# The factors for the first rows of W2 are loaded into f's blocks instead of W1's q tiles, and two of them one pass later

## The chip, the core and the metric

The kernel runs on one core of a Trainium2 chip. The metric is the time of one execution on the device in microseconds (us): 2252.89 us for the kernel before, the median of three runs (2249.2 to 2253.3). The profile comes from one execution of its own, of 2253.21 us.

## What is computed

One layer of an encoder trunk for a sequence of 512 rows of 2048 float32 values: an input projection, two kinds of attention (a window with grouped keys, and a dilated one), an output projection, a layer norm, and the part that this case is about:

```python
h = layer_norm(ALPHA * h + mix, ln1_g[i], ln1_b[i])
ff = jnp.square(jax.nn.relu(h @ w1[i])) @ w2[i]
ple = (p[i] @ w_ple[i]) * jax.nn.sigmoid(h @ w_ple_gate[i])
h = layer_norm(ALPHA * h + ff + ple, ln2_g[i], ln2_b[i])
```

W1 has 2048 x 8192 elements, W2 has 8192 x 2048.

## The kernel before

Products with large weights are made in float32r with a split: of each operand a high part (a copy that ScalarE rounds, `wh`, `sh`) and a low part (what VectorE finds left over, `wl`, `sl`), and three matmuls high x high, low x high, high x low.

**Passes and steps.** From the gate's projection on, every product of 512 x 1024 outputs is made by Strassen's scheme with seven products, `strassen` (L602 to L674): two passes for the gate, eight for W1 (chunk n = 0 to 7 of 1024 columns of f), eight for W2 (m = 0 to 3 for the rows of W2, c = 0 and 1 for the halves of its columns). A pass has 28 steps, each a pair (p, k): product p of the seven, and k, a quarter of its depth. `STEPS` sets their order: steps 0 to 11 are products 1, 5 and 6, steps 12 to 19 products 3 and 7 in turn, steps 20 to 27 products 2 and 4. Each step splits one weight tile of 128 x 1024 (`w_split`, L598 on ScalarE and L599 on VectorE) and makes 12 matmuls with it (L668, L670, L671). For product 5 VectorE first forms a difference of two weight tiles (L634) and from it product 6's tile (L635), for 3 and 7 one more (L622), for 4 one more (L617).

**Factors.** The other operand of step (p, k) is a *factor*, `sg[k // 2][p]`: half g = k // 2 of product p, split into high and low (`put`: L532 on ScalarE, L533 on VectorE) and kept for the whole pass. For W1 they are made from h and serve all eight passes. For W2 they are made from f: `squared`, which is called two steps after a quarter of a W1 chunk is complete, puts relu's square into a block f, forms three differences and a sum in place on VectorE (L738 to L745) and stores seven blocks of 512 KB to a DRAM tensor `s_d` (L733, three on ScalarE's queue and four on POOL's). `f_factors(m, ...)` loads those of chunks 2m and 2m + 1 again, 14 blocks per m, each with one DMA on SP's queue (L584) and one split. For a new m the loads are put between the steps of the pass before (the last W1 pass for m = 0, else pass c = 1 of m - 1), two steps behind the last use of the old factor, since a factor has two buffers per product, one for each half; those of products 2 and 4, which are used last, are put into the new m's first pass by the table `LATE`.

**Rings.** All these tiles come from a few rings, whose tags give the number of buffers:

```python
WB = {"r": 4, "q": 2, "k": 4, "wh": 3, "wl": 3, "c": 3, "g": 4}
LATE = {2: (12, 16), 4: (14, 18)}
```

A weight tile for product 5's difference and one for 3's and 7's go through `q`, two buffers (L592 with tag q; from the second W2 pass on, `hold`, they are kept in `g` instead). The f blocks go through `g`, four buffers, and so do a few tiles of the gate's passes. In the kernel before, the loads of factors, `block("qs", "q")`, go through `q`.

**Order.** The text of the program gives the order of steps; a scheduler then orders the instructions on each engine by when it expects them to be ready. Each engine and each DMA queue works through its own list in order, so that an instruction that waits holds all behind it. SP's queue carries the weight tiles of rings r, q and g and the factors; POOL's carries ring k's weights, four of the stores of f's blocks and, in W2, the sums into `z_d`.

Of the kernel before, what the change touches and what calls it, by code (L numbers as in the profile page):

```python
# [38 lines left out]
def block_kernel(ctx: ExitStack, tc: tile.TileContext, xT, pT, positions, w_in, w_o, w_gate, w_ple,  # L39
# [47 lines left out]
    def unit(src, acts, nk=16, mid=None):  # L87
        o = bank()
        for g in range(nk // 8):
            raw = raw_load(src[:, g * 1024:(g + 1) * 1024])  # L90
            for p in range(2):
                piece_mm(o, raw[:, p * 512:(p + 1) * 512], acts, 8 * g + 4 * p, nk)
            if g == 0 and mid:
                mid()
        return o
# [74 lines left out]
    def rope_split(o):  # L170
        raw = t_f("qr", "q")
        nc.scalar.activation(raw, o, AF.Copy)
        sw = t_f("sw", "q", F32, 32)
        nc.vector.stream_shuffle(sw, raw[:32], swap)
        nc.vector.tensor_tensor(sw, sw, sinr, op=ALU.mult)
        nc.vector.tensor_tensor(raw[:32], raw[:32], cosr, op=ALU.mult)
        nc.vector.tensor_tensor(raw[:32], raw[:32], sw, op=ALU.add)
        return split(raw, "q", "q")
# [150 lines left out]
    for h in range(8):  # L329
# [22 lines left out]
        q = rope_split(unit(w[1], x_hl, 16, q_mid))  # L352
# [167 lines left out]
    def w_tile(name, tag, shape=(P, 1024), dt=F32):  # L520
        return wp.tile(list(shape), dt, name=name, tag=tag, bufs=WB[tag])
# [4 lines left out]
    def block(name, tag="g"):  # L526
        return w_tile(name, tag, (P, 4, HS))

    def put(sg, p, src):
        hi = sp.tile([P, 4, HS], R32, name=f"s{p}h", tag=f"s{p}h", bufs=2)  # L530
        lo = sp.tile([P, 4, HS], R32, name=f"s{p}l", tag=f"s{p}l", bufs=2)
        nc.scalar.activation(hi, src, AF.Copy)  # L532
        nc.vector.tensor_tensor(lo, src, hi.bitcast(F32), op=ALU.subtract)  # L533
        sg[p] = hi, lo

    def h_factors(g, sg):

        q = {}

        def get(*ks):  # L540
            for i in ks:
                th, kh = i // 2, i % 2
                k0 = 8 * kh + 4 * g
                q[i] = block("qh")
                nc.sync.dma_start(q[i], h_d[k0:k0 + 4, :, th * HS:(th + 1) * HS].rearrange("k p t -> p k t"))

        def a1():
            get(0, 2, 3)
            put(sg, 1, q[0])

        def a2():
            nc.vector.tensor_tensor(q[3], q[3], q[2], op=ALU.add)
            put(sg, 5, q[3])

        def a3():
            nc.vector.tensor_tensor(q[3], q[3], q[0], op=ALU.subtract)
            put(sg, 6, q[3])

        def b1():
            get(1)  # L560
            put(sg, 2, q[1])

        def b2():
            get(0, 2)
            nc.vector.tensor_tensor(q[2], q[0], q[2], op=ALU.subtract)
            put(sg, 7, q[2])

        def b3():
            get(3)
            nc.vector.tensor_tensor(q[1], q[1], q[3], op=ALU.subtract)  # L570
            nc.vector.tensor_tensor(q[1], q[1], q[2], op=ALU.add)
            put(sg, 3, q[1])

        return [a1, a2, a3], [b1, b2, b3, lambda: put(sg, 4, q[3])]

    def f_factors(m, sg):


        at = {False: {}, True: {}}
        for p in range(1, 8):  # L580
            for g in range(2):
                def step(p=p, g=g):
                    x = block("qs", "q")
                    nc.sync.dma_start(x, s_d[2 * m + g, p - 1])  # L584
                    put(sg[g], p, x)
                late = p in LATE
                at[late].setdefault(LATE[p][g] if late else STEPS.index((p, 2 * g + 1)) + 2, []).append(step)
        return at

    def w_load(src, tag):  # L590
# [105 lines left out]
    early, late = zip(*(h_factors(g, sh[g]) for g in range(2)))  # L696
# [20 lines left out]

    sf = [{}, {}]
    at = f_factors(0, sf)
    for n in range(NFC):  # L720
        f = {}
# [86 lines left out]
    for m in range(NM):  # L808
        more = m < NM - 1
        late = at[True]  # L810
        if more:
            nsf = [{}, {}]
            at = f_factors(m + 1, nsf)
        for c in range(2):
            def read(p, b, c=c):
                e = pair("ev")
                nc.scalar.activation(e, b, AF.Copy)  # L817
                nc.gpsimd.dma_start(z_d[READ[p][0], 2 * c + READ[p][1]], e, accum_op=ALU.add)
            mid = late if c == 0 else at[False] if more else {}
            strassen(lambda k, q, m=m, c=c: w2[m, c, q, k], sf, read if more else last_sum(c), m + c > 0, mid,  # L820
                     STEPS if more or c == 0 else ENDS)
        if more:
            sf = nsf
# [6 lines left out]
STEPS = ((1, 0), (1, 1), (5, 0), (1, 2), (5, 1), (1, 3), (5, 2), (6, 0), (5, 3), (6, 1), (6, 2), (6, 3),  # L830
         (3, 0), (7, 0), (3, 1), (7, 1), (3, 2), (7, 2), (3, 3), (7, 3),
         (2, 0), (4, 0), (4, 1), (2, 1), (4, 2), (4, 3), (2, 2), (2, 3))
LATE = {2: (12, 16), 4: (14, 18)}
# [97 lines left out]
```

## Time and profile before

| what | value |
|---|---|
| median of three runs | 2252.89 us |
| the profiled execution | 2253.21 us, of which the span of instructions 2251.4 us |
| TensorE matmuls | 2144.6 us busy, 95% of the span |
| VectorE | 1608.7 us, 71% |
| ScalarE | 1060.3 us, 47% |
| POOL | 124.3 us, 6% |
| last W1 pass (n = 7) | 1480.75 to 1577.19 us, 96.44 us |
| first W2 pass (m = 0, c = 0) | 1577.19 to 1663.13 us, 85.94 us |
| W1 pass n = 6, for comparison | 1399.95 to 1480.75 us, 80.80 us |

Times are read from the start of the span. The busy time of TensorE is modelled at the end of each matmul, so that what counts is when it starts and where it sits idle. A timeline row gives the start, the length, the engine, the line, the operation and its tiles, and in brackets the idle time of the engine just before it with what ended it. A pass begins with the first matmul on `s1h`.

### The profile page before, as it was taken

The page shows a single profiled execution, that of the slowest core. Times are in us where ns is not written, and L with a number is a line of the kernel's source. Part 1 is how long each engine was busy: PE and PEld are TensorE (multiplying, and loading weights), DVE is VectorE, ACT ScalarE, POOL GpSimd, SP SyncE. Part 2 cuts the span into 40 slices and gives each one's busy share as a digit, 9 for nine tenths or more (in the row PEclk, how much of TensorE's full clock was granted, in tenths as well). Part 3 has the DMA queues.
Part 4 walks back from the last instruction along what each step waited for, and adds up shares of the span by engine and source line. Part 5 has one row for each costly group of instructions (what it writes and reads, how often), then busy time and mean ns, then how long its engine had stood idle before and what let it go on. Part 6 is the DMA issues. An engine that isn't in the chain of part 4 may idle for free.

```text
span 2251.4 us, 26067 instructions
## 1 busy us (share of the span) xinstructions
PE 2144.6 (95%) x9672; PEld 1760.2 (78%) x9672; DVE 1608.7 (71%) x1945; ACT 1060.3 (47%) x1372; POOL 124.3 (6%) x192
## 2 busy tenths in 40 slices
PE   8999999999995699999999999999999999999995
PEld 7888888888884488888888888877777777887784
DVE  7666655566375888776876877777777776777787
ACT  5554444443234444455555455455455455455331
POOL 0000000000003000000000000000011011101000
PEclk9999999999998799999999999999999999999998
DMA  6222222233325875665575566567779679679562
GB/s 226 76 66 75 77 74 85 75 108 128 107 94 185 273 272 194 216 216 196 196 239 174 195 215 202 196 210 235 260 198 282 178 206 279 180 212 294 170 243 103
DMA packets 125696, 405.80 MB, mean 180 GB/s; under 512 B 13152, under 2 KB 24416, under 8 KB 125568
## 3 DMA queue, kind: packets, MB, share of 16 engines
q1 hardware_dynamic: 89696, 289.71, 38.2%
q0 software_dynamic: 23584, 85.06, 13.7%
q10 hardware_dynamic: 12288, 29.36, 3.8%
q8 instruction: 76, 1.25, 0.2%
q14 instruction: 52, 0.43, 0.1%
HBM read 333.82 MB, written 70.25 MB: 179 GB/s over the span
## 4 chain that ended last, share of the span: by engine, by line
PE 76%; DMA 9%; DVE 9%; issue 4%; ACT 2%; DVEq 0%; SPq 0%; ACTq 0%
PE u L71 9%; PE u L72 9%; PE u L73 9%; PE a L668 9%; PE a L670 8%; PE a L671 8%; PE b L671 4%; DVE wl L599 4%; PE b L668 4%; PE b L670 4%; DMA wr<-in_w 4%; PE c L671 2%; PE c L668 2%; PE c L670 2%; DMA qs<-s_d 2%
## 5 line engine op out<-in xcount | busy, mean ns | idle before, releaser
L598 ACT ACTIVATE wh<-wr 128x1024 fp32r<-128x1024 f32 x288 | 303.8, 1059 | 357.9 <-PE a L670 198.8
L599 DVE TENSOR_TENSOR wl<-wr,wh 128x1024 fp32r<-128x1024 f32 x288 | 350.9, 1220 | 111.0 <-ACT wh L598 111.0
L64 ACT ACTIVATE wh<-raw 128x512 fp32r<-128x512 f32 x216 | 135.7, 629 | 283.9 <-PE u L72 271.1
L65 DVE TENSOR_TENSOR wl<-raw,wh 128x512 fp32r<-128x512 f32 x216 | 150.9, 699 | 161.0 <-ACT wh L64 129.3
L598 ACT ACTIVATE wh<-wk 128x1024 fp32r<-128x1024 f32 x144 | 152.5, 1060 | 182.5 <-PE a L670 95.8
L71 PE MATMUL u<-xh,wh 128*128 128x512 f32 x576 | 227.8, 396 | 5.8 <-ACT xh L64 5.8
L72 PE MATMUL u<-xl,wh 128*128 128x512 f32 x576 | 225.8, 392 | 0.0
L73 PE MATMUL u<-xh,wl 128*128 128x512 f32 x576 | 225.7, 392 | 0.0
L599 DVE TENSOR_TENSOR wl<-wk,wh 128x1024 fp32r<-128x1024 f32 x144 | 175.4, 1222 | 62.0 <-ACT wh L598 61.8
L617 DVE TENSOR_TENSOR wk<-wr,wk 128x1024 f32<-128x1024 f32 x72 | 88.1, 1224 | 90.5 <-DMA wr<-in_w 83.5
L668 PE MATMUL a<-wh,s1h 128*128 128x512 f32 x288 | 114.7, 398 | 31.4 <-ACT wh L598 31.2
L71 PEld LDWEIGHTS u<-xh,wh 128*128 128x128 f32 x576 | 108.9, 189 | 27.3 <-ACT xh L64 5.8
L73 PEld LDWEIGHTS u<-xh,wl 128*128 128x128 f32 x576 | 108.8, 189 | 22.7
L72 PEld LDWEIGHTS u<-xl,wh 128*128 128x128 f32 x576 | 108.9, 189 | 22.0 <-DVE xl L65 0.4
L668 PE MATMUL b<-wh,s5h 128*128 128x512 f32 x288 | 116.3, 404 | 8.4 <-ACT wh L598 8.4
L671 PE MATMUL b<-wl,s5h 128*128 128x512 f32 x288 | 117.1, 407 | 7.3 <-DVE wl L599 7.3
L668 PE MATMUL a<-wh,s6h 128*128 128x512 f32 x288 | 113.8, 395 | 4.9 <-ACT ev L817 2.8
L671 PE MATMUL b<-wl,s3h 128*128 128x512 f32 x288 | 113.2, 393 | 5.0 <-DVE wl L599 4.9
L671 PE MATMUL c<-wl,s2h 128*128 128x512 f32 x288 | 113.2, 393 | 4.9 <-DVE wl L599 4.7
L668 PE MATMUL a<-wh,s7h 128*128 128x512 f32 x288 | 113.0, 392 | 4.4 <-ACT wh L598 4.1
L671 PE MATMUL a<-wl,s1h 128*128 128x512 f32 x288 | 113.7, 395 | 2.4 <-DVE wl L599 2.4
L670 PE MATMUL b<-wh,s5l 128*128 128x512 f32 x288 | 115.6, 401 | 0.0
(243 smaller groups left out, 4934.8 us busy)
## 6 DMA issues: line engine op xcount, KB each, us to landing
wr<-in_w SPq DMA_DIRECT2D x196, 512.0 KB, 3.9
wq<-in_w SPq DMA_DIRECT2D x72, 512.0 KB, 3.8
raw<-in_w_in SPq DMA_DIRECT2D x64, 512.0 KB, 3.7
wk<-in_w POOLq DMA_DIRECT2D x64, 512.0 KB, 5.6
qs<-s_d SPq DMA_DIRECT2D x56, 512.0 KB, 4.9
z_d<-ev POOLq DMA_DIRECT2D x42, 512.0 KB, 7.3
raw<-in_w_o SPq DMA_DIRECT2D x32, 512.0 KB, 3.5
s_d<-f POOLq DMA_DIRECT2D x32, 512.0 KB, 4.3
```

What stands on the lines that cost most here:

```text
L64: nc.scalar.activation(hi, src, AF.Copy)
L65: nc.vector.tensor_tensor(lo, src, hi.bitcast(F32), op=ALU.subtract)
L71: nc.tensor.matmul(o, wh, ah, start=start, stop=False)
L72: nc.tensor.matmul(o, wh, al, start=False, stop=False)
L73: nc.tensor.matmul(o, wl, ah, start=False, stop=stop)
L598: nc.scalar.activation(hi, t, AF.Copy)
L599: nc.vector.tensor_tensor(lo, t, hi.bitcast(F32), op=ALU.subtract)
L617: nc.vector.tensor_tensor(t4[k], get(b21, k, 2, "r"), t2[k], op=ALU.subtract)
L668: nc.tensor.matmul(o, sh[:, i, x], wh[:, c], start=first and k == 0 and j == 0, stop=False, skip_group_check=skip)
L670: nc.tensor.matmul(o, sl[:, i, x], wh[:, c], start=False, stop=False, skip_group_check=skip)
L671: nc.tensor.matmul(o, sh[:, i, x], wl[:, c], start=False, stop=k == 3 and j == 1, skip_group_check=skip)
```

## The change

Two things change in `f_factors`. For m = 0 the 14 loads go through ring `g`, the four buffers of f's blocks, and no longer through `q`; for m = 1 to 3 they go through `q` as before. And for m = 0 and half g = 1, products 3 and 7 join the table of late loads: of this half four products (2, 3, 4, 7) are now loaded within the first W2 pass, of the other half two as before. So two loads move from the last W1 pass (steps 20 and 21 of it) to steps 3 or 4 and 6 of the first W2 pass.

```diff
@@ -580,11 +580,12 @@
         for p in range(1, 8):
             for g in range(2):
                 def step(p=p, g=g):
-                    x = block("qs", "q")
+                    x = block("qs", "q" if m else "g")
                     nc.sync.dma_start(x, s_d[2 * m + g, p - 1])
                     put(sg[g], p, x)
-                late = p in LATE
-                at[late].setdefault(LATE[p][g] if late else STEPS.index((p, 2 * g + 1)) + 2, []).append(step)
+                plan = LATE if m or g == 0 else {**LATE, 3: (3, 4), 7: (3, 6)}
+                late = p in plan
+                at[late].setdefault(plan[p][g] if late else STEPS.index((p, 2 * g + 1)) + 2, []).append(step)
         return at
```

**SP's queue, start of the last W1 pass.** Names end in the number of their buffer: wq_11705, 11751, 11799 and 11843 are product 5's second tiles for k = 0 to 3, wr_11648 to 11773 product 1's tiles, qs_11727 the factor (1, g = 0), qs_11793 (5, 0), qs_11821 (1, 1), wr_11929 and 11972 product 3's tiles. Before:

```order
L592 DMA wr_11575<-in_w1 128x1024
L584 DMA qs_11727<-s_d_5213 128x1024
L592 DMA wr_11648<-in_w1 128x1024
L592 DMA wr_11687<-in_w1 128x1024
L592 DMA wr_11733<-in_w1 128x1024
L592 DMA wr_11773<-in_w1 128x1024
L592 DMA wq_11751<-in_w1 128x1024
L592 DMA wr_11929<-in_w1 128x1024
L584 DMA qs_11793<-s_d_5213 128x1024
L592 DMA wq_11799<-in_w1 128x1024
L592 DMA wr_11972<-in_w1 128x1024
L584 DMA qs_11821<-s_d_5213 128x1024
```

The same place with the change:

```order
L593 DMA wr_11575<-in_w1 128x1024
L593 DMA wq_11751<-in_w1 128x1024
L593 DMA wr_11648<-in_w1 128x1024
L593 DMA wr_11687<-in_w1 128x1024
L593 DMA wr_11733<-in_w1 128x1024
L593 DMA wr_11773<-in_w1 128x1024
L593 DMA wq_11799<-in_w1 128x1024
L593 DMA wr_11929<-in_w1 128x1024
L593 DMA wq_11843<-in_w1 128x1024
L584 DMA qs_11727<-s_d_5213 128x1024
L593 DMA wr_11972<-in_w1 128x1024
L584 DMA qs_11793<-s_d_5213 128x1024
```

Every weight tile of ring q moved up by one place in that ring (wq_11751 stands where the first factor stood), and the first factor moved behind all of product 5's tiles.

**ScalarE, the last W1 pass from step 3 on.** wh_11757, 11805 and 11849 belong to steps (5,1), (5,2) and (5,3), wh_11775 to (1,3), wh_11827 to (6,0). Before:

```order
L532 ACTIVATE s1h_11729<-qs_11727 128x1024
L598 ACTIVATE wh_11757<-wr_11687 128x1024
L598 ACTIVATE wh_11775<-wr_11773 128x1024
L598 ACTIVATE wh_11805<-wr_11733 128x1024
L532 ACTIVATE s5h_11795<-qs_11793 128x1024
L598 ACTIVATE wh_11827<-wk_11707 128x1024
```

With the change:

```order
L599 ACTIVATE wh_11757<-wr_11687 128x1024
L599 ACTIVATE wh_11775<-wr_11773 128x1024
L532 ACTIVATE s1h_11729<-qs_11727 128x1024
L599 ACTIVATE wh_11805<-wr_11733 128x1024
L599 ACTIVATE wh_11827<-wk_11707 128x1024
L532 ACTIVATE s5h_11795<-qs_11793 128x1024
```

The first factor's copy moved back by two weight copies and now stands directly ahead of that of step (5,2).

**ScalarE, the first W2 pass.** wh_12451 belongs to step (5,2), wh_12467 to (6,0), `ev` is the copy of product 1's sums out of PSUM, which must be done before product 6 adds to the same bank. Before:

```order
L598 ACTIVATE wh_12451<-wr_12384 128x1024
L598 ACTIVATE wh_12467<-wk_12364 128x1024
L532 ACTIVATE s2h_12561<-qs_12559 128x1024
L817 ACTIVATE ev_12442<-a_12302 128x1024
L598 ACTIVATE wh_12489<-wr_12424 128x1024
```

With the change:

```order
L532 ACTIVATE s3h_12392<-qs_12390 128x1024
L599 ACTIVATE wh_12451<-wr_12372 128x1024
L599 ACTIVATE wh_12467<-wk_12352 128x1024
L532 ACTIVATE s7h_12441<-qs_12439 128x1024
L532 ACTIVATE s2h_12561<-qs_12559 128x1024
L818 ACTIVATE ev_12436<-a_12290 128x1024
```

Three copies of factors instead of one now stand ahead of `ev`, one of them ahead of step (5,2)'s weights.

## Rows read from the trace of the kernel before

**Rows 1.** The page: TensorE's busy time, and the chain that ended last, by engine.

```profile
PE 2144.6 (95%) x9672; PEld 1760.2 (78%) x9672; DVE 1608.7 (71%) x1945; ACT 1060.3 (47%) x1372; POOL 124.3 (6%) x192
PE 76%; DMA 9%; DVE 9%; issue 4%; ACT 2%; DVEq 0%; SPq 0%; ACTq 0%
```

**Rows 2.** Busy time by stretch: whole passes, then their steps 0-11 and 12-19.

```profile
core 0: us, PE busy (x) PEld busy (x) DVE busy (x) ACT busy (x) POOL busy (x), PEclk, DMA share, GB/s
1399.95:1480.75 80.80, 79.96 (x370) 66.30 (x368) 59.52 (x52) 41.48 (x45) 4.25 (x8) 1.00 0.60 202
1480.75:1577.19 96.44, 87.38 (x370) 68.85 (x368) 71.53 (x62) 50.15 (x55) 4.25 (x8) 0.95 0.67 224
1577.19:1663.13 85.94, 81.47 (x346) 65.54 (x344) 61.10 (x53) 40.55 (x41) 9.55 (x14) 0.96 0.82 254
...
1399.95:1433.48 33.53, 33.53 (x153) 27.85 (x152) 28.36 (x25) 16.61 (x18) 2.13 (x4) 1.00 0.58 205
1433.48:1457.09 23.61, 22.77 (x105) 18.68 (x104) 17.33 (x15) 10.59 (x11) 0.00 (x0) 1.00 0.52 165
1480.75:1522.69 41.94, 37.78 (x154) 29.45 (x152) 30.92 (x27) 19.78 (x21) 2.14 (x4) 0.92 0.61 207
1522.69:1553.17 30.48, 25.58 (x103) 19.35 (x102) 23.76 (x21) 15.46 (x17) 0.00 (x0) 0.94 0.64 206
1577.19:1616.68 39.49, 36.72 (x153) 29.87 (x152) 30.72 (x27) 18.38 (x20) 3.90 (x6) 0.91 0.84 280
1616.68:1641.37 24.69, 22.99 (x98) 17.66 (x96) 17.66 (x16) 11.88 (x13) 1.47 (x2) 1.00 0.67 208
1780.76:1804.33 23.57, 22.08 (x98) 17.94 (x96) 12.28 (x11) 10.32 (x11) 1.33 (x2) 1.00 0.62 179
```

**Rows 3.** Timeline of TensorE: the longest stalls of the two passes.

```profile
1500.26 0.64 PE L668 MATMUL b<-wh,s5h 128*128 128x512 f32 x1 [2.05 <-ACT wh L598]
...
1548.30 0.79 PE L668 MATMUL a<-wh,s7h 128*128 128x512 f32 x1 [2.08 <-ACT wh L598]
...
1600.05 0.79 PE L668 MATMUL a<-wh,s6h 128*128 128x512 f32 x1 [2.77 <-ACT ev L817]
```

**Rows 4.** Timeline of VectorE, last W1 pass: what it waited for.

```profile
1497.83 1.23 DVE L634 TENSOR_TENSOR wr<-wq,wr 128x1024 f32<-128x1024 f32 x1 [3.84 <-DMA wq<-in_w]
...
1545.85 1.23 DVE L622 TENSOR_TENSOR wq<-wr,wq 128x1024 f32<-128x1024 f32 x1 [1.57 <-DMA wq<-in_w]
```

**Rows 5.** Timeline of SP's queue, last W1 pass: DMAs as they are issued.

```profile
1478.00 0.33 SPq L592 DMA_DIRECT2D wq<-in_w  x1
...
1484.93 0.33 SPq L584 DMA_DIRECT2D qs<-s_d  x1
1490.61 0.33 SPq L592 DMA_DIRECT2D wq<-in_w  x1
```

**Rows 6.** Timeline of ScalarE's queue and POOL: stores of f's blocks.

```profile
1486.60 0.33 ACTq L733 DMA_DIRECT2D s_d<-f  x1
...
1492.01 0.53 POOL L733 DMA_DIRECT2D s_d<-f  x1 [1.74 <-DVE f L745]
```

**Rows 7.** DMA issues from 1486 to 1501: number, KB each, median us to landing.

```profile
s_d<-f POOLq DMA_DIRECT2D x3, 512.0 KB, 7.9
s_d<-f ACTq DMA_DIRECT2D x1, 512.0 KB, 4.7
wq<-in_w SPq DMA_DIRECT2D x1, 512.0 KB, 7.2
...
qs<-s_d SPq DMA_DIRECT2D x1, 512.0 KB, 3.2
```

**Rows 8.** Timeline of ScalarE, first W2 pass: the wait ahead of product 1's copy.

```profile
1598.03 1.06 ACT L532 ACTIVATE s2h<-qs 128x1024 fp32r<-128x1024 f32 x1 [5.25 <-DMA qs<-s_d]
1598.99 1.00 ACT L817 ACTIVATE ev<-a 128x1024 f32<-128x1024 f32 x1
```

**Rows 9.** DMA issues from 1588 to 1592: the load of that factor, median us to landing.

```profile
qs<-s_d SPq DMA_DIRECT2D x1, 512.0 KB, 7.6
```

## The prediction

> **What bounds the kernel now.** I read the page first: TensorE is busy for 95% of the span and holds 76% of the chain that ended last [rows 1]. So a change gains only where TensorE sits idle or runs at a lower clock. The second view is the busy time by stretch, cut at the passes [rows 2]: the W1 pass n = 6 takes 80.80 us, the last W1 pass, in which ten factors for W2 are loaded, 96.44 us, and the first W2 pass 85.94 us. All three have the same 28 steps. Cut further, the loss sits in four stretches. Steps 0 to 11 take 33.53 us in n = 6, 41.94 us in the last W1 pass (8.41 more) and 39.49 us in the first W2 pass (5.96 more). Steps 12 to 19 take 23.61 us in n = 6 and 30.48 us in the last W1 pass (6.87 more); in the first W2 pass 24.69 us against 23.57 us two passes later (1.12 more). Together 22.36 us: all that these loads can cost.
>
> The loss is half waiting, half clock. In the last W1 pass TensorE is busy for 37.78 of the 41.94 us, and its granted clock is 0.92 on average, against 1.00 in n = 6 [rows 2]: part of the time it runs at the lower of the two levels, 1.2 GHz instead of 2.4, and the matmuls that begin behind the long stalls are recorded at 0.64 to 0.79 us each [rows 3]. At a mean of 0.92, some 3.4 us of the 41.94 (8%) are lost to the clock, beside 4.2 us of idle time.
>
> The third view, the timelines, says what is late. TensorE waits for weight copies by ScalarE (2.05 us at step (5,2), 2.08 at (7,3), the two longest of that pass) [rows 3]; behind them VectorE waits for tiles of ring q, 3.84 and 1.57 us [rows 4]. These come late because factors sit in that ring of two: SP issues the q tile for (5,2) only at 1490.61, 5.7 us behind the factor ahead of it [rows 5], since it needs the buffer of the first factor, which VectorE has only then split. In the first W2 pass the stall is of another kind: step (6,0) waits 2.77 us for the copy of product 1's sums [rows 3], which stands on ScalarE behind the copy of a factor whose load it waits for, 5.25 us [rows 8].
>
> **The change, part by part.** No instruction and no byte is added; the same 14 loads and splits are made, some in another place.
>
> *Steps 12 to 19 of the last W1 pass.* The factors of products 3 and 7 alternate with W1's q tiles in two buffers there; now they take g's. SP can issue the q tiles for (7,0) and (7,1) before their steps. What remains is VectorE's load: 21 instructions in 23.76 us of busy time before, 15 in n = 6 [rows 2]; two factors move away, so 19. At 17.33 / 15 = 1.16 us each that is 22.0 us, under the 23.61 us that TensorE needs, but with little to spare. I take 24.1 us: a gain of 6.4 us. Bounds: 0 (VectorE's order makes the same stalls) and 6.9.
>
> *Steps 0 to 11 of the last W1 pass.* The q tiles now come first: the one for (5,2) is issued at 1478.00, where the one for (5,1) was [rows 5], the one for (5,3) at about 1484.9, where a factor was. Those two waits go. But the first factor now needs a buffer of ring g, and all four hold f blocks of n = 6. The first to be free is the block of quarter (0,0): its store leaves ScalarE's queue at 1486.60 and takes 4.7 us [rows 6, 7]. So the factor is issued at 1491.3, no longer ahead of product 5's tiles. How long it takes is bounded by the rows of the same window: 3.2 us (the fastest factor) to 7.9 us (the stores); I take the q tile's 7.2, issued at 1490.61 among the same stores [rows 7]. It lands at 1498.5. On ScalarE its copy now stands directly ahead of that of step (5,2)'s weights: 1.05 us each, done by 1499.6 and 1500.6. VectorE then makes the factor's low part (to 1500.9), a sum for product 6 (to 1502.0) and only then the low part for (5,2), to 1503.2, at 1.2 us each as in rows 4, some overlapped. In n = 6's rhythm (5,2) would start at 1498.2 (1500.26 less the 2.05 of idle time [rows 3]) and want the low part two matmuls later, at 33.53 / 153 = 0.22 us each [rows 2]: at 1498.7. So it is 4.5 us late, a little more than the idle time of this stretch before (4.2), in one piece instead of several. For the clock I take 2.6 us instead of 3.4, since there is one recovery instead of two. 4.5 + 2.6 = 7.1 against 8.41: a gain of 1.3 us. With a landing in 3.2 us everything is 4 us earlier and the low part 0.5 us late, and the gain is up to 7.7; with 7.9 us and the two further factors late as well I put the lower end at a loss of 2.
>
> The next loads follow the other stores: the last leaves POOL at 1492.01 and needs 7.9 us by the median [rows 6, 7], so the fourth factor is issued at about 1500. Behind it on SP stand the q and r tiles for products 3 and 7, and step 12 began at 1522.69 before [rows 2]: some 20 us cover them. If that cover goes, the stall is TensorE's, at step (7,0).
>
> *First W2 pass.* The weights that the next pass keeps in ring g were loaded early and crowded its steps 0 to 11 with DMAs (a share of 0.84 [rows 2]); now factors take these buffers first and the weights come later, still long before their pass. But three factor copies instead of one stand ahead of product 1's copy on ScalarE, and their loads wait, as above, for the stores of n = 7's f blocks. The third of them is issued at the time of the one in rows 8 (it needs the same store's landing as a weight tile did), so product 1's copy ends near 1600 as before; the first one delays (5,2)'s low part by some 2 us, but within the same wait. I take 0.8 us of gain here (bounds: a loss of 3, three copies of 1.05 us in a row; a gain of 5.96) and 0.7 us of the 1.12 in steps 12 to 19, where the q ring is free of factors: 1.5 us.
>
> *Sum.* 6.4 + 1.3 + 1.5 = 9.2 us off the profiled execution's 2253.2 (its span is 2251.4): 2244.0 us. The median of the runs, 2252.89, lies 0.3 below it, which I leave out. What can be told from no change is 0.2%, 4.5 us: below 2248.4 is faster, above 2257.4 slower.
>
> **Where a rule of the notes speaks otherwise.** Rows 7 show 7.2 to 7.9 us for 512 KB while stores and loads run together. The Trainium skill, "DMA: Bandwidth & Descriptors", section "Anatomy of one DMA — SWDGE (gpsimd) path", fits a DMA by 2.0 us and its bytes at 436 GB/s; for 512 KB that is 3.2 us (an estimate by that page). The fastest factor here took 3.2 us too [rows 7], but alone; under the stores the trace does not agree.
>
> **The rivals.**
> *Short landings.* If the loads took the 3.2 us of the fastest factor [rows 7] even beside the stores, the first part would give 7.7 us, and in the first W2 pass the factor ahead of product 1's copy would land in 3.2 instead of 7.6 us [rows 9], 4.4 earlier, which is more than the 2.77 us that (6,0) waited [rows 3]; 5.96 and 0.7 us would go there. 6.4 + 7.7 + 6.7 = 20.8: 2232.4 us. For it: the contending weight loads of ring g are gone. Against it: the stores are still there. 0.14. (This is what the fit in the paragraph above would make of it.)
>
> *The early wait eats the rest.* VectorE has no slack in steps 12 to 19 (22.0 of 23.6 us), and if the pass enters them late and with its queue out of step, only 2 to 4 us of the 6.4 are left, and the early part loses 2: 0 to 4 us in all, 2249.2 to 2253.2. For it: VectorE's busy time is the same, 71.53 us in the last W1 pass. 0.18.
>
> *Slower: copies at the head of ScalarE's queue.* One factor copy that waited for its load cost 5.96 us in the first W2 pass [rows 2, 8], clock and all. Now each load waits for a store, and four copies (in steps 3 to 9 of the last W1 pass) and five (steps 4 to 11 of the first W2 pass) can do this. I count one of each. From the fourth such stall on the change loses: 4 x 5.96 = 23.8 against the 22.36 that all this cost before; five give 29.8, that is 7.4 us more, 2260.6 us. Against it: later loads are issued 5 us and more apart from use. 0.08.
>
> **How the numbers follow.** The forecast, 9.2 us with the bounds of its early part, is 2238 to 2248: 0.60. Short landings 0.14, eaten 0.18, slower 0.08. Faster is the first two, 0.74; same 0.18; slower 0.08. The likeliest gives 2244.0. The range goes from 2236 to 2252: below it lies some 0.10 (most of the short landings), above it 0.10 (the slower case and the last of the eaten one).
>
> **What would show it.** In the profile after: the last W1 pass should take 88 to 89 us, the first W2 pass 84 to 85. VectorE's waits for q tiles [rows 4] should be gone from the last W1 pass, the first factor's load be issued near 1491 and land some 7 us later, and step (5,2) be the longest stall, with a wait of ScalarE for that load ahead of it. The (7, k) stalls should be under 1 us each. It is wrong if the (7, k) stalls remain, if (5,2) starts on time, or if the first W2 pass grows past 86 us.

## The result, and the profile after

The changed kernel takes 2240.01 us (median of 6 runs, 2233.37 to 2242.92) against 2253.10 us (6 runs, 2249.20 to 2254.47) of the kernel before on the same chip: a ratio of 0.9941, 95% interval 0.9927 to 0.9956. That is 13.1 us, or 0.6%, faster. The forecast was 2244.0 us; the time lies inside its range, but the gain is 1.4 times what the sum said (13.1 against 9.2 us).

The profiled execution took 2239.67 us. Lines behind the edited ones stand one further down than before (L598 is now L599). The page's first part and its chain, to be held against [rows 1]:

```profile
PE 2139.2 (96%) x9672; PEld 1758.8 (79%) x9672; DVE 1606.4 (72%) x1945; ACT 1061.1 (47%) x1372; POOL 124.2 (6%) x192
PE 74%; DMA 10%; DVE 9%; issue 4%; ACT 2%; DVEq 0%; SPq 0%; ACTq 0%
```

No instruction was added or taken away on any engine. Where the time went is in the busy time by stretch: last W1 pass, first W2 pass, then steps 0 to 11 and 12 to 19 of the one and of the other [rows 2]:

```profile
core 0: us, PE busy (x) PEld busy (x) DVE busy (x) ACT busy (x) POOL busy (x), PEclk, DMA share, GB/s
1482.72:1568.60 85.88, 82.02 (x369) 67.38 (x368) 68.42 (x60) 48.62 (x53) 4.26 (x8) 0.98 0.70 239
1568.60:1649.50 80.90, 78.42 (x345) 63.54 (x344) 63.10 (x55) 42.79 (x43) 9.55 (x14) 1.00 0.89 283
1482.72:1522.30 39.58, 35.72 (x153) 28.84 (x152) 34.00 (x30) 21.10 (x23) 2.14 (x4) 0.96 0.75 268
1522.30:1544.86 22.56, 22.56 (x105) 18.77 (x104) 20.80 (x19) 12.94 (x13) 0.00 (x0) 1.00 0.64 208
1568.60:1605.22 36.62, 34.32 (x153) 27.64 (x152) 33.79 (x31) 22.17 (x24) 3.90 (x6) 1.00 0.92 313
1605.22:1627.74 22.52, 22.34 (x97) 17.87 (x96) 16.92 (x16) 10.32 (x11) 1.33 (x2) 1.00 0.84 272
```

The two passes fall from 96.44 and 85.94 us to 85.88 and 80.90. In steps 12 to 19 of the last W1 pass TensorE is busy for the whole 22.56 us. All that is left in that pass is two stalls at step (5,2), and the chain behind them is the one that had been worked out. SP's queue issues the first factor at 1493.10 (the pass starts 2 us later than before), ScalarE waits for it 7.24 us with step (5,2)'s weight behind it, VectorE makes the factor's low part, product 6's sum and then step (5,2)'s low part, and TensorE waits twice. The timelines of SP's queue, ScalarE, VectorE and TensorE:

```profile
1493.10 0.33 SPq L584 DMA_DIRECT2D qs<-s_d  x1
...
1500.08 1.06 ACT L532 ACTIVATE s1h<-qs 128x1024 fp32r<-128x1024 f32 x1 [7.24 <-DMA qs<-s_d]
1501.04 1.04 ACT L599 ACTIVATE wh<-wr 128x1024 fp32r<-128x1024 f32 x1
...
1501.17 1.23 DVE L533 TENSOR_TENSOR s1l<-qs,s1h 128x1024 fp32r<-128x1024 f32 x1 [4.11 <-ACT s1h L532]
1502.31 1.22 DVE L636 TENSOR_TENSOR wk<-wk,wr 128x1024 f32<-128x1024 f32 x1
1503.45 1.22 DVE L600 TENSOR_TENSOR wl<-wr,wh 128x1024 fp32r<-128x1024 f32 x1
...
1502.13 0.50 PE L669 MATMUL b<-wh,s5h 128*128 128x512 f32 x1 [2.00 <-ACT wh L599]
...
1504.72 0.50 PE L672 MATMUL b<-wl,s5h 128*128 128x512 f32 x1 [1.85 <-DVE wl L600]
...
1505.74 0.63 PE L672 MATMUL b<-wl,s5h 128*128 128x512 f32 x1
```

The last of these rows is one of eight matmuls behind the stall that ran at the lower clock, 1.2 GHz: each starts some 0.42 us after the one before it, elsewhere 0.23.

VectorE's waits for q tiles (single ones in [rows 4]) are gone. The rows give what it waited for, the total, the number and the longest in us. In the last W1 pass of the kernel before it waited for q tiles at two lines:

```profile
DVE wr L634 <- DMA wq<-in_w: 5.8, 2, 3.8
DVE wq L622 <- DMA wq<-in_w: 3.2, 3, 1.6
```

Its three longest waits in that pass now:

```profile
DVE wl L600 <- ACT wh L599: 12.6, 9, 3.3
DVE s1l L533 <- ACT s1h L532: 4.1, 1, 4.1
DVE wk L618 <- DMA wr<-in_w: 0.4, 1, 0.4
```

In the first W2 pass three factor copies stand ahead of product 1's copy `ev`, as foreseen, and `ev` begins 21.82 us after the start of the pass (1590.42 - 1568.60); before it was 21.80 (1598.99 - 1577.19) [rows 8]. Step (6,0) starts 22.88 us after the start of the pass, before 22.86; its stall of 2.77 us [rows 3] has gone, and in its place stand two at (5,2), of 0.44 and 1.85 us. ScalarE's timeline:

```profile
1584.39 1.06 ACT L532 ACTIVATE s3h<-qs 128x1024 fp32r<-128x1024 f32 x1 [5.67 <-DMA qs<-s_d]
...
1588.18 1.06 ACT L532 ACTIVATE s7h<-qs 128x1024 fp32r<-128x1024 f32 x1 [0.83 <-DMA qs<-s_d]
1589.46 1.06 ACT L532 ACTIVATE s2h<-qs 128x1024 fp32r<-128x1024 f32 x1 [0.22 <-DMA qs<-s_d]
1590.42 1.01 ACT L818 ACTIVATE ev<-a 128x1024 f32<-128x1024 f32 x1
```

Still the pass took 5.0 us less, where 1.5 had been forecast: 2.9 us in steps 0 to 11, all behind the start of (6,0), where TensorE ran at the lower clock before and does not now, and 2.2 in steps 12 to 19. Either the program does better there, or this execution was a good one.

### The profile page after: what moved, and what is told of

It is laid out like the page before. It is cut to its first block, busy times and chain, and to the rows that moved or that the text cites. A ratio compares the mean times of both kernels' runs of the same rounds, so it can differ in the third digit from the quotient of the medians.

```text
span 2237.9 us, 26062 instructions
## 1 busy us (share of the span) xinstructions
PE 2139.2 (96%) x9672; PEld 1758.8 (79%) x9672; DVE 1606.4 (72%) x1945; ACT 1061.1 (47%) x1372; POOL 124.2 (6%) x192
## 4 chain that ended last, share of the span: by engine, by line
PE 74%; DMA 10%; DVE 9%; issue 4%; ACT 2%; DVEq 0%; SPq 0%; ACTq 0%
PE u L73 9%; PE u L72 9%; PE u L71 9%; PE a L669 8%; PE a L672 8%; PE a L671 8%; DVE wl L600 5%; DMA wr<-in_w 4%; PE b L672 4%; PE b L671 3%; PE b L669 3%; DMA qs<-s_d 3%; PE c L672 2%; PE c L669 2%; PE c L671 2%
## 5 line engine op out<-in xcount | busy, mean ns | idle before, releaser
L599 ACT ACTIVATE wh<-wr 128x1024 fp32r<-128x1024 f32 x288 | 304.1, 1059 | 352.7 <-PE a L671 207.1
L599 ACT ACTIVATE wh<-wk 128x1024 fp32r<-128x1024 f32 x144 | 152.7, 1060 | 185.2 <-PE a L671 97.6
L669 PE MATMUL c<-wh,s2h 128*128 128x512 f32 x288 | 114.3, 397 | 0.9 <-ACT wh L599 0.9
```

The lines of the kernel that those rows point to most:

```text
L599: nc.scalar.activation(hi, t, AF.Copy)
L669: nc.tensor.matmul(o, sh[:, i, x], wh[:, c], start=first and k == 0 and j == 0, stop=False, skip_group_check=skip)
```

## The experiments

Theory: what pays is the ring. The weights' q tiles no longer share two buffers with tiles that wait for a store, a load and a split. What is left over is a load's wait at the head of ScalarE's queue. Rivals: the move of two loads by a pass carries the gain (the first expectation of ring only speaks of four factors; the change moves two, of products 3 and 7 of the second half); or the small first W2 pass is a draw of one execution.

All eleven kernels in one table, three of them run twice. Ratios are to runs of the kernel before beside them on the same chip, with 95% intervals; rows come from several chips, on which the kernel before had medians of 2251.32 to 2253.86 us, so that ratios and not medians are to be compared. The four stretches are in us, from the busy time by stretch of the one profiled execution of each row.

| kernel | median us | ratio | last W1 pass, 0-11 | 12-19 | first W2 pass, 0-11 | 12-19 |
|---|---|---|---|---|---|---|
| before | 2253.10 | | 41.94 | 30.48 | 39.49 | 24.69 |
| before, again | 2250.56 | 0.9991 [0.9978, 1.0003] | 42.51 | 29.24 | 38.29 | 25.55 |
| changed | 2240.01 | 0.9941 [0.9927, 0.9956] | 39.58 | 22.56 | 36.62 | 22.52 |
| changed, again | 2240.51 | 0.9940 [0.9925, 0.9955] | 37.83 | 22.56 | 36.98 | 25.15 |
| ring only | 2237.26 | 0.9945 [0.9932, 0.9957] | 40.71 | 22.56 | 37.01 | 23.31 |
| ring only, again | 2237.45 | 0.9938 [0.9922, 0.9954] | 37.14 | 22.56 | 36.49 | 23.66 |
| late places only | 2251.10 | 1.0001 [0.9990, 1.0011] | 41.81 | 29.15 | 38.20 | 24.86 |
| before, one copy behind | 2253.28 | 0.9994 [0.9982, 1.0006] | 40.19 | 29.35 | 33.53 | 30.99 |
| changed, one copy behind | 2237.60 | 0.9942 [0.9929, 0.9955] | 36.00 | 22.56 | 37.60 | 25.07 |
| changed, copies behind (a) | 2233.39 | 0.9929 [0.9917, 0.9942] | 35.94 | 24.22 | 33.57 | 21.76 |
| changed, copies behind (b) | 2233.24 | 0.9909 [0.9892, 0.9927] | 33.53 | 25.31 | 36.57 | 21.76 |
| changed, copies behind (c) | 2233.71 | 0.9910 [0.9892, 0.9928] | 34.97 | 23.71 | 39.05 | 21.76 |
| changed, copies behind (d) | 2233.48 | 0.9914 [0.9895, 0.9933] | 33.72 | 24.54 | 33.75 | 22.78 |
| ring only, copies behind | 2232.00 | 0.9916 [0.9898, 0.9933] | 33.53 | 24.13 | 33.53 | 21.76 |

**The same kernels again.** The changed kernel and the one before, unchanged, each for a second profile. On record for the changed one:

> The changed kernel itself, for a second profile of the same program. My theory: the first W2 pass was 80.9 us in one profile and 84.4 us in a kernel that does not differ in it, because landings and the granted clock there differ from one execution to the next; so here it lies anywhere from 80.5 to 85 us, the last W1 pass at 84 to 88 us, and the time at 2236 to 2241 us. Rival (the 80.9 us belongs to the program: the smaller stall keeps the clock whole each time): 80.6 to 81.4 us with the granted clock at 1.00.

and for the one before:

> The kernel before itself, for a second profile. My theory: the last W1 pass is 94 to 97 us again (93.6 to 96.4 in three kernels that share the ring of two there), the first W2 pass 84.5 to 87 us; so the change is worth about 11 us in the one and, against 80.9 to 84.4 us in the changed kernel, 2 to 4 us in the other. Rival (the 96.4 us was a bad draw): 92 us or less.

The time repeats (2240.51 us; 2250.56 us), the first W2 pass does not. The second profile of the changed kernel, first W2 pass, then its steps 0 to 11 and 12 to 19; and of the kernel before, last W1 pass and first W2 pass:

```profile
1568.47:1652.36 83.89, 78.54 (x345) 63.51 (x344) 63.14 (x55) 42.73 (x43) 9.58 (x14) 1.00 0.86 273
1568.47:1605.45 36.98, 34.44 (x154) 27.62 (x152) 31.86 (x29) 22.20 (x24) 3.91 (x6) 1.00 0.91 306
1605.45:1630.60 25.15, 22.34 (x97) 17.86 (x96) 18.93 (x17) 10.21 (x11) 1.34 (x2) 1.00 0.76 242
```

```profile
1481.84:1577.59 95.75, 84.30 (x370) 66.64 (x368) 71.40 (x62) 49.78 (x55) 4.27 (x8) 0.98 0.65 225
1577.59:1663.19 85.60, 80.09 (x346) 64.57 (x344) 61.21 (x53) 40.66 (x41) 9.57 (x14) 0.98 0.82 255
```

The same program took 80.90 us in this pass, then 83.89, and a kernel that does not differ in it ("changed, one copy behind") 84.43. So the 80.90 was a good draw, and one profile of each kernel says too much about this pass. The theory named landings and the clock; between the two profiles it was not the clock, which is 1.00 in both. The difference lies in steps 12 to 19, where TensorE has one stall of 2.65 us in a step of product 3 (none over 0.18 us in the first profile). It waited for a low part from VectorE, which had stood idle for 3.50 us two operations earlier; what held VectorE up the rows do not say. VectorE and TensorE in the second profile:

```profile
1615.67 1.22 DVE L623 TENSOR_TENSOR wq<-wr,wq 128x1024 f32<-128x1024 f32 x1 [3.50 <-issue]
...
1619.59 0.50 PE L672 MATMUL b<-wl,s3h 128*128 128x512 f32 x1 [2.65 <-DVE wl L600]
```
With two profiles each, the last W1 pass loses 11.1 us (96.44 and 95.75 against 85.88 and 84.13) and the first W2 pass 3.4 (85.94 and 85.60 against 80.90 and 83.89). All the rest of the span (less the two passes) spread from 2067.6 to 2071.1 us in these four profiles.

**Ring only**: the changed kernel without the late places (steps 4 and 6 of the first W2 pass).

```diff
-                plan = LATE if m or g == 0 else {**LATE, 3: (3, 4), 7: (3, 6)}
+                plan = LATE
```

> Only the ring is changed; products 3 and 7 of the second chunk keep their places at the end of the last W1 pass. My theory (what pays is that the factors of the last W1 pass no longer take turns with the weights' blocks in the ring of two): the last W1 pass is as with the whole change in steps 0 to 11 (about 39.6 us) and 12 to 19 (22.6 us), and the first W2 pass lies between 81 and 86 us, since other copies (of product 2's and 4's factors) now stand ahead of the weight's copy of step (5,2) and of product 1's. In all 2240 to 2246 us. Rival (the four factors moved a chunk later carry the gain, because at their old place they wait for f's blocks in the same ring): the end of the last W1 pass grows by 4 us or more, and the time is 2247 us or above.

And a second time:

> The kernel with only the ring changed, once more, for a second profile and a second set of times. My theory: as the whole change within what two measurements of one kernel differ by, 2235 to 2241 us; last W1 pass 84 to 88 us, first W2 pass 81 to 84.5 us. Rival (the late move costs, and the ring alone is the better kernel): 2237 us or less again, with the interval of the ratio below that of the whole change.

2237.26 and 2237.45 us; the first lies below the 2240 to 2246 that I had written, and the second last W1 pass, 83.44 us, just below its 84 to 88. The ratios lie on both sides of the changed kernel's. The rival's growth at the end of the last W1 pass is not there: steps 20 to 27 took 23.74 us in both profiles, as with the change. The whole gain is the ring's. The medians are 2.6 to 3.3 us below the changed kernel's, but the kernel before had lower medians beside them too (2251.32 and 2251.53 us against 2253.10 and 2253.86), and the intervals of the ratios overlap widely. That the late places cost something is not shown, only that no gain of theirs can be seen.

Ring g has four buffers where q has two, and in it the factors still take turns, with f's blocks and the next pass's weights. A ring q with more buffers for both kinds was not run, so it is not shown whether the number of buffers or the separation from W1's weights pays.

**Late places only**: the changed kernel with every factor in ring q.

```diff
-                    x = block("qs", "q" if m else "g")
+                    x = block("qs", "q")
```

> Only the late places are changed; every factor of the first chunks stays in the ring of two. My theory: the last W1 pass stays at 94 to 97 us (before 96.4), because the factors of products 1, 5, 6, 3 and 7 still take turns with the weights there; the first W2 pass changes by -5 to +2 us against 85.9; in all 2246 to 2254 us. Rival (the late move carries the gain): about 2240 us.

2251.10 us, a ratio of 1.0001. The last W1 pass took 94.96 us, and VectorE waits for q tiles (formed into differences at L635 and L623) as in the kernel before. Its waits in that pass:

```profile
DVE wr L635 <- DMA wq<-in_w: 5.7, 2, 3.5
DVE wq L623 <- DMA wq<-in_w: 3.6, 4, 1.8
```

**Before, one copy behind.** Here and below a factor's copy is pinned to a place on ScalarE's queue: its load stays at its step, but the split is written some steps later (`HOLD`, product and half to steps) and its ScalarE copy is kept in the order of the text, so that the scheduler cannot pull it forward.

```diff
+        (tc.keep_in_program_order if kept else lambda x: x)(nc.scalar.activation(hi, src, AF.Copy))
...
+                at[late].setdefault(n, []).append(lambda step=step, x=x: x.append(step()))
+                at[late].setdefault(n + hold, []).append(lambda p=p, g=g, x=x: put(sg[g], p, x[0], True))
...
+HOLD = {(2, 0): 3}
```

> The kernel before, with one thing changed: in the first W2 pass the copy of product 2's factor stands behind product 1's copy out of its bank (it waited 5.25 us ahead of it). My theory: steps 0 to 11 of that pass fall from 39.5 us to 34 to 37 us and nothing else gains, so the time falls by 2 to 5 us against the kernel before. Rival (in a ring of two a factor that is copied later keeps its buffer longer and the weights behind it come late): what is gained in steps 0 to 11 is lost in 12 to 27, within 1 us of the kernel before or slower.

Half of the theory held, and the rival decided. Steps 0 to 11 of the first W2 pass fell to 33.53 us, without a stall, and all of it came back in steps 12 to 19, at 30.99 us. The factor's buffer comes free later: its low part is made by 1613.55, and the q tile for step (7,1) is issued at 1613.58; VectorE waits 3.96 us for it and TensorE 3.59. ScalarE, VectorE, SP's queue, then VectorE and TensorE (in this kernel and in those below, `strassen`'s lines stand some eight further down):

```profile
1611.04 1.05 ACT L532 ACTIVATE s2h<-qs 128x1024 fp32r<-128x1024 f32 x1
...
1612.33 1.22 DVE L533 TENSOR_TENSOR s2l<-qs,s2h 128x1024 fp32r<-128x1024 f32 x1
...
1608.79 0.33 SPq L584 DMA_DIRECT2D qs<-s_d  x1
1613.58 0.33 SPq L600 DMA_DIRECT2D wq<-in_w  x1
...
1618.65 1.23 DVE L630 TENSOR_TENSOR wq<-wr,wq 128x1024 f32<-128x1024 f32 x1 [3.96 <-DMA wq<-in_w]
...
1621.10 0.50 PE L676 MATMUL a<-wh,s7h 128*128 128x512 f32 x1 [3.59 <-ACT wh L606]
```

So with this place of the copy the wait only moves. But the copy went further back than the expectation says: it starts 35.4 us after the start of the pass (1611.04 - 1575.66), behind the copies of products 1, 5 and 6 out of their banks, where it stood 20.8 us after it before. A place directly behind product 1's copy, which would keep the buffer for less time, was not run.

**Changed, one copy behind**: `HOLD = {(1, 0): 4}`, which does no more on ScalarE than set the first factor's copy behind step (5,2)'s weight.

> The whole change, with one ScalarE copy moved: that of the first factor (product 1, first chunk) goes behind the copy of step (5,2)'s weight. My theory: (5,2) then starts on time, and the stall moves to (6,0), which waits for product 1's copy out of its bank, still behind the second factor's copy (its load lands at about 1503.6 us): (6,0) starts 2.2 us earlier than with the change (23.8 us after the start of the pass instead of 26.0), so steps 0 to 11 of the last W1 pass take 37 to 38 us instead of 39.6, and the time is 2.0 to 2.6 us below the changed kernel's. Rival (what holds (5,2) is VectorE or the weight's own load): no difference from the changed kernel, 2240 us.

Step (5,2) starts on time, and TensorE waits 1.63 us at (6,0) for product 1's copy, which stands behind the second factor's copy. (6,0) starts 21.72 us after the start of the pass (1504.43 - 1482.71), earlier than the 23.8 I had written, since the second factor landed at 1501.5 here. ScalarE and TensorE:

```profile
1497.65 1.06 ACT L532 ACTIVATE s1h<-qs 128x1024 fp32r<-128x1024 f32 x1 [0.55 <-DMA qs<-s_d]
1498.62 1.04 ACT L606 ACTIVATE wh<-wk 128x1024 fp32r<-128x1024 f32 x1
1501.46 1.06 ACT L532 ACTIVATE s5h<-qs 128x1024 fp32r<-128x1024 f32 x1 [1.80 <-DMA qs<-s_d]
1502.43 1.04 ACT L606 ACTIVATE wh<-wr 128x1024 fp32r<-128x1024 f32 x1
1503.37 1.00 ACT L695 ACTIVATE c<-a 128x1024 f32<-128x1024 f32 x1
...
1504.43 0.50 PE L676 MATMUL a<-wh,s6h 128*128 128x512 f32 x1 [1.63 <-ACT c L695]
```

Steps 0 to 11 took 36.00 us, 1 us better than I had written (the four profiles of the changed kernel and of ring only, which work in the same order there, have 37.14 to 40.71). The 2.0 to 2.6 us that I expected of the time cannot be seen: a ratio of 0.9942 against 0.9941 and 0.9940.

**Changed, copies behind.** Four versions of the same idea, in which also later copies go behind the copies that TensorE waits for. (a) `HOLD = {(1, 0): 6, (5, 0): 5, (1, 1): 2, (3, 1): 8, (7, 1): 6, (2, 0): 2}`:

> The whole change, with the early factors' ScalarE copies (products 1 and 5 in the last W1 pass; products 3, 7 and 2 in the first W2 pass) moved behind the weight copies and behind product 1's copy out of its bank. My theory: no load of a factor stands ahead of work that TensorE waits for, so steps 0 to 11 take 33.6 to 35 us in both passes (39.6 and 36.6 with the change), both passes end at about 80 to 82 us, and the time is 2231 to 2234 us. Rival (the ring: copies later keep its buffers longer, so the loads behind them stand on SyncE's queue and the weights behind those come late): stalls for weights on SyncE's queue at steps 7 to 12, and 2238 to 2245 us.

2233.39 us, as the theory said, and the first W2 pass ran without one stall, in 77.09 us. In the last W1 pass a factor that was not held, product 5's of the second half, now came to stand ahead of weights and waited 4.64 us, and its steps 0 to 11 took 35.94 us, over the 35 I had set.

(b) `HOLD = {(1, 0): 4, (5, 0): 3, (3, 1): 8, (7, 1): 6, (2, 0): 2}`:

> As the kernel with all copies behind, but in the last W1 pass the first factor's copy of each chunk stands a little earlier: the first one behind (5,2)'s weight copy, the second behind product 1's copy out of its bank, both of product 5 behind product 5's copy. My theory: steps 0 to 11 of the last W1 pass take 33.6 to 35.5 us, 12 to 19 take 22.6 to 23.5 us (less low-part work is left for them than with all copies behind), the first W2 pass 77.1 to 78.5 us; time 2230 to 2234 us. Rival (a factor's load that lands late still blocks the queue, now ahead of (6,0)): steps 0 to 11 at 36 us or more, time 2234 to 2238 us.

Steps 0 to 11 of the last W1 pass took 33.53 us, without a stall. Steps 12 to 19 (25.31 us) and the first W2 pass (80.09) were worse than expected: in the latter product 4's factor, which is not held, waited ahead of step (6,1)'s weight. ScalarE and TensorE:

```profile
1590.13 1.06 ACT L532 ACTIVATE s4h<-qs 128x1024 fp32r<-128x1024 f32 x1 [5.50 <-DMA qs<-s_d]
1591.10 1.99 ACT L606 ACTIVATE wh<-wk 128x1024 fp32r<-128x1024 f32 x2
...
1595.11 0.50 PE L679 MATMUL a<-wl,s6h 128*128 128x512 f32 x1 [2.18 <-DVE wl L607]
```

(c) `HOLD = {(1, 0): 6, (5, 0): 5, (1, 1): 4, (5, 1): 3, (3, 1): 8, (7, 1): 6, (2, 0): 2}`:

> As the kernel with all copies behind, but all four copies of products 1 and 5 stand behind product 5's copy out of its bank. In the kernel before it a product 5 factor that was not held waited 4.64 us at the head of the queue ahead of (6,1)'s weight. My theory: that wait goes, steps 0 to 11 of the last W1 pass take 33.5 to 34.5 us, steps 12 to 19 take 22.6 to 25 us, since six low parts are now left to VectorE in a row; first W2 pass 77.1 to 78.5 us; time 2229 to 2234 us. Rival (buffers kept longer push the loads behind them on SyncE's queue): weights late from step 12 on, 25 us or more there, time 2234 us or above.

2233.71 us. The early stretch took 34.97 us, a little over what was expected, and the first W2 pass missed by 4 us: product 4's copy stands as in (b) and waited 6.74 us, and steps 0 to 11 took 39.05 us.

(d) As (b), with `(4, 0): 2` added:

> As the kernel with one factor ahead in the last W1 pass, with product 4's factor of the first chunk also moved behind product 5's copy in the first W2 pass, where it waited 5.50 us at the head of the queue ahead of (6,1)'s weight. My theory: the 2.46 us of stalls at (6,0) go, steps 0 to 11 of the first W2 pass take 33.5 to 34.5 us (36.6 in that kernel), the time is 2229 to 2233 us. Rival (what was late there was the weights' own load: VectorE also waited 2.04 us for one): 35.5 us or more, and no gain against 2233 us.

Steps 0 to 11 of the first W2 pass took 33.75 us: the stall was product 4's copy. The time, 2233.48 us, is over the 2233 that I had set and not below (b)'s; between these four it can't be told which is best. Steps 12 to 19 of the last W1 pass are longer in all four (23.7 to 25.3 us) than with the change (22.56). More splits are left to them, 20 or 21 operations of VectorE instead of 19, which is the likely reason.

**Ring only, copies behind**: `plan = LATE` and `HOLD = {(1, 0): 4, (5, 0): 3, (2, 0): 2, (4, 0): 2}`.

> The ring changed, products 3 and 7 of the second chunk kept at their old place, and the copies of products 1, 5, 2 and 4 moved behind the copies that TensorE waits for. My theory (the late move pays nothing, the places of the copies do): steps 0 to 11 take 33.5 to 36 us in both passes, the time is 2231 to 2235 us, as with the late move. Rival (with the copies in good places, the late move is what lets the end of the last W1 pass go through): steps 20 to 27 of the last W1 pass take 25 us or more (23.7 with the change), the time 2236 us or above.

2232.00 us, without the late places. Last W1 pass and first W2 pass, and their steps 0 to 11:

```profile
1485.31:1566.64 81.33, 80.29 (x369) 66.22 (x368) 70.41 (x62) 50.16 (x55) 4.27 (x8) 1.00 0.75 265
1566.64:1643.69 77.05, 77.05 (x345) 63.89 (x344) 60.80 (x53) 40.67 (x41) 9.58 (x14) 1.00 0.90 284
1485.31:1518.84 33.53, 33.53 (x153) 27.86 (x152) 32.71 (x29) 20.89 (x23) 2.14 (x4) 1.00 0.80 303
1566.64:1600.17 33.53, 33.53 (x153) 27.85 (x152) 28.87 (x26) 18.26 (x19) 3.91 (x6) 1.00 0.90 298
```

Both stretches are at the 33.53 us of W1's pass n = 6 [rows 2], the clock is whole, and the rival's growth in steps 20 to 27 is not there (23.67 us). Of what these loads cost in the four stretches, 1.6 us are left: 24.13 us in steps 12 to 19 of the last W1 pass, against 22.55 in an undisturbed pass (below). This and (b) to (d) are faster than both kernels. Where the changed kernel was run beside (b) and (c), it took 2240.51 us against 2233.24 and 2233.71, and the intervals of their ratios (0.9892 to 0.9928) hardly touch its own (0.9925 to 0.9955). Ring only, run again beside (d) and this kernel, took 2235.89 to 2241.52 us; (d)'s runs lie below that (2227.01 to 2235.36), and this kernel's all but one (2230.57 to 2235.99). The medians are 4.0 and 5.5 us apart.

## Why the prediction was right, and where its sum was off

The direction and the mechanism were right, and of the places only the stall in the first W2 pass moved, from (6,0) to (5,2); every term was taken too small. The signs came: no q tile is waited for in the last W1 pass, no (7,k) stall is left there, and (5,2) waits behind ScalarE's wait for the first factor. The passes were shorter than forecast: 85.88 and 84.13 us instead of 88 to 89, and 80.90 and 83.89 instead of 84 to 85. Gains by stretch, as means of two profiles of each kernel:

| step of the prediction | forecast | measured | by which profiles |
|---|---|---|---|
| last W1 pass, steps 12 to 19 | 6.4 | 7.3 | 30.48, 29.24 to 22.56, 22.56 |
| last W1 pass, steps 0 to 11 | 1.3 | 3.5 | 41.94, 42.51 to 39.58, 37.83 |
| first W2 pass, steps 0 to 11 | 0.8 | 2.1 | 39.49, 38.29 to 36.62, 36.98 |
| first W2 pass, steps 12 to 19 | 0.7 | 1.3 | 24.69, 25.55 to 22.52, 25.15 |
| sum | 9.2 | 14.2 | median of the runs: 13.1 |

- **Steps 12 to 19 of the last W1 pass: right, with a wrong yardstick.** The q tiles came in time and no stall is left. "What remains is VectorE's load", 22.0 us under the 23.61 that TensorE needs: VectorE took 20.80 us for its 19 operations, 1.09 each instead of 1.16. And TensorE does not need 23.61: that was pass n = 6, in which it sat idle for 0.84 of them [rows 2]. In an undisturbed W1 pass of the kernel before, n = 2, the same steps take 22.55 us:

```profile
1113.45:1136.00 22.55, 22.55 (x105) 18.75 (x104) 17.62 (x16) 10.20 (x10) 0.00 (x0) 1.00 0.56 177
```

So the upper bound of 6.9 us was too low as well.

- **Steps 0 to 11 of the last W1 pass: right in the chain, off in its sizes.** The first factor issued 10.4 us after the start of the pass (forecast 10.5), landed 7.0 us later (7.2 taken), its copy blocked step (5,2)'s weight, and the low part came as listed. The low part came 4.3 us late where 4.5 were forecast (TensorE was to start on it at about 1500.4 and did at 1504.72), and the clock cost about 1.6 (eight matmuls that start 0.42 instead of 0.23 us apart) where 2.6 were taken. So the size that was off in this profile is the clock's. In the second profile the factor was issued 10.5 us after the start and copied at 1499.92, 5.1 us behind its issue, and the stretch took 37.83: there the landing was shorter than taken, too. That the copy at the head of the queue makes this loss is shown: with the copies of products 1 and 5 moved behind, the stretch takes 33.53 us in two kernels.

- **First W2 pass: the time of `ev` was right, the clock was not.** `ev` started 21.82 us into the pass as forecast (21.80). But "I take 0.8 us of gain" kept the clock's loss of before; in both profiles of the change it was 1.00 in steps 0 to 11, against 0.91 and 0.96 before. Nothing in the prediction says why it should stay whole, and in "changed, one copy behind", which works in the same order there, it fell to 0.95 and the stretch took 37.60 us: this part of the gain is partly luck. The reason given, that fewer DMAs crowd these steps, did not come: their DMA share rose from 0.84 to 0.92. Steps 12 to 19 are unsure: 22.52, 25.15, and 25.07 us in that other kernel.

- **The rivals.** Short landings: not so short. In the changed kernel the first factor took 7.0 and 5.1 us from its issue to its copy, in the other kernels with the new ring whose copy waited for it 4.1 to 7.0. The Trainium skill, "DMA: Bandwidth & Descriptors", section "Anatomy of one DMA — SWDGE (gpsimd) path", fits a DMA on that path, issued by GpSimd, by a fixed 2.0 us and its bytes at 436 GB/s, which is 3.2 us for 512 KB by an estimate from that page. Loads on SP's queue among the stores of these steps do not agree with it. Five factor loads took 7.0 us by the median, in the DMA issues of 1488 to 1503 after the change:

```profile
qs<-s_d SPq DMA_DIRECT2D x5, 512.0 KB, 7.0
```

The early wait that eats the rest: no, VectorE has room in steps 12 to 19, 20.80 of 22.56 us. Slower by copies at the head of ScalarE's queue: the mechanism is real, and copies placed further back win some 7 us (2240.51 against 2233.24 and 2233.71), but it was one costly wait in each pass, not the four from which the change would have lost.

What the prediction did not see is that half of the change is idle: it spoke of both parts as one, and the late places alone or on top of the ring gave nothing that can be measured. Its count for steps 12 to 19 of the last W1 pass ("two factors move away, so 19") needs the late places by its words; with the ring alone VectorE has 19 operations in these steps too, and TensorE takes the same 22.56 us.

## What to carry to other kernels

Tiles with different lives should not take turns in a short ring: a factor that waits for a store, a load and a split held up weights that were only waiting for a buffer. With two buffers the one later place that was tried for a copy on ScalarE moved the wait without a gain, while with the other ring later places gave 4 to 7 us. An operation that waits for a load stands at the head of its engine's queue with all that is behind it, so it belongs behind what the busiest engine needs next, also where its own result is not urgent. And where a forecast rests on one pass as a yardstick or one profile as the outcome, look at a second: here an unchanged pass differed by 3 us between two executions.

## What the runs showed of the hardware

Much the same idle time of TensorE cost the clock in one execution and not in another, with ScalarE and VectorE working in the same order. In steps 0 to 11 of the last W1 pass stalls of 0.23 and 1.85 us at step (5,2) went with a granted clock of 0.95 (second profile of the changed kernel), 0.70 and 1.85 us at the same step with 1.00 (ring only, again). In the first W2 pass 0.44 and 1.85 us left it at 1.00 in the changed kernel, and 1.85 us alone went with 0.95 in "changed, one copy behind". The stretches of the second profile of the changed kernel, of ring only, again, and of "changed, one copy behind":

```profile
1484.34:1522.17 37.83, 35.74 (x154) 28.87 (x152) 34.01 (x30) 21.14 (x23) 2.14 (x4) 0.95 0.76 280
```

```profile
1480.79:1517.93 37.14, 34.50 (x153) 27.61 (x152) 33.49 (x30) 20.98 (x23) 2.14 (x4) 1.00 0.78 284
```

```profile
1564.91:1602.51 37.60, 35.70 (x153) 28.85 (x152) 33.21 (x30) 22.19 (x24) 3.90 (x6) 0.95 0.91 306
```

So a price for the clock that is taken from one stall in one execution does not carry over to another.

A load of the same 512 KB from the same place, issued 10.4 to 11.2 us into the same pass beside the same stores, landed 4.1 to 7.0 us later in eight profiles, read from the start of the copy that waited for it. What sets this was not tried.
